# One pool of buffers, a more cautious planner, and another order of blocks in a two-layer encoder trunk

## The chip, the cores and the metric

The kernel runs on one core of a Trainium2 chip. Its work is issued to TensorE (PE: matmuls; PEld: their weight loads), VectorE (DVE), ScalarE (ACT) and SyncE (SP), which issues nearly all DMAs. GpSimd (POOL) does next to nothing. Each engine executes its instructions in the order in which they were written for it, and waits where an instruction's input or buffer isn't ready. The metric is device microseconds of one execution, as the median of several runs.

## The reference

`x` is (256, 2048) in float32, and there are two layers. Per layer (weights differ by layer):

```python
shift, scale, gate = split(c @ w_ada + b_ada, 3)          # c: (2048,), w_ada: (2048, 6144)
h = rms_norm(x, g_pre) * (1 + scale) + shift
u, g_pool, q, k, v, g_diff = split(h @ w_in)              # w_in: (2048, 6144), each part 1024 wide
pool_out = multiscale_pool(u, w_pool, pool_scale) * silu(g_pool)   # trailing means over 2, 4, 8, 16 tokens, 4 groups
q, k = rope(q), rope(k)
p = softmax(mask(q @ k.T / 8))                            # 8 heads, 2 maps each, chunks of 64 tokens
att = (p[0] - lam * p[1]) @ v
diff_out = rms_norm(att, subln_g) * (1 - lam_init) * silu(g_diff)
y = concat(pool_out, diff_out) @ w_out                    # w_out: (2048, 2048)
x = x + (1 + gate) * rms_norm(y, g_post)
```

All weights are float32 and are read once: about 50 MB of `w_ada`, 50 MB of `w_in` and 17 MB of `w_out` for each layer.

## The kernel before

**Products.** Each float32 operand is split into a high part (rounded to the matmul's format, `hi`) and a rest (`lo`), and a product is made of three matmuls, hi x hi, hi x lo and lo x hi. The unit of work is a piece of 256 rows of contraction by 512 columns of `w_in` or `w_out` (`Unit`, 512 KB): two 128-row halves, times two halves of the 256 tokens, times three matmuls, which is 12 matmuls of 128 x 512. For each unit SP loads `raw`, ACT casts `hi` (`cast`), and DVE subtracts to get `lo` (`rest`); tiles in the profile are `rawz`, `whiz`, `wloz`. The blocks of 512 columns of `w_in` are numbered 0 to 11: U 0 and 1, the pool's gate GP 2 and 3, Q 4 and 5, K 6 and 7, V 8 and 9, the attention's gate GD 10 and 11. GP blocks are computed turned (features on the partitions), in matmuls of 256 columns.

**The conditioning.** `w_ada` is no matmul: each half row tile of 128 x 1024 (`adaz`, 512 KB, 192 in all) is multiplied by the spread `c` and summed along the row by one DVE instruction (`ada`). When the sums of a column tile are there, `ab` makes A (the factor) and B (the summand) of `h` for it, and ACT writes the modulated `h` from the transposed, scaled `xn` (`make_h`; `half_h` for the first ones of a layer, by halves of the tokens). The contraction is in eight pairs of column tiles ("k pairs"), and `w_in` products can use a k pair only when its h is there.

**The plan.** `plan` lays out the units: a block is visited with as many k pairs as are then available, the partial sum is saved to SBUF and copied back into PSUM at the next visit (`prepare`: `accc<-zz` in the profile), and the blocks end in the order in which they complete, to which `ORDERS` gives their numbers. `w_out` goes through its four column blocks with one half of the contraction and then with the other (`HALVES`); contraction tiles 0 to 7 (k pairs 0 to 3) are the pool's outputs and 8 to 15 the attention's. `START` says how many k pairs of h a layer begins with, which also forces their `w_ada` tiles in ahead of it; `TURN` says how many first units are regrouped so that they are done for the first half of the tokens and then for the second.

**The order on the engines.** No loop runs on the chip: Python threads (`Task`) each write a part of the program, and `Flow` decides whose instruction comes next. It has a model of each engine's clock (`COST`: fixed, per element, for an accumulating output, until visible), of the DMA link (`MB_US`, `LANDING`, `FIRST`) and of TensorE's slow start (`COLD`). `next_of` takes, for an engine, the waiting instruction with the earliest due time among those that could start at once by the model:

```python
rows.append((t.due(), max(self.now[k], a.dep), us, t))
rows.sort(key=lambda r: r[:2])
```

Products are due at 1e9, after everything else; a transpose, a pool or an attention step is due some us ahead of the unit that needs it (`need`, `need_h`, `need_cat`). All instructions are recorded in helper line 126, so groups in the profile are told apart by tile names.

**Buffers.** There are 34 buffers of 128 x 1024 floats ("z") for `raw`, `hi`, `lo`, `w_ada` tiles, saved sums, h and cat; 12 of 128 x 512 ("t") for temporaries: xn and the unsplit h, the rotated q and k, the probabilities, their transposes, the pool's; and one of 128 x 2048 ("g") that holds `w_pool` and then the spread gate G. `Slots.take` waits in the plan until enough are free and takes the one that was last used longest ago. The instruction that first writes it then waits on the chip for the last user.

Of the kernel before, what the change touches and what calls it, by code (L numbers as in the profile page):

```python
# [130 lines left out]
class Flow:  # L131
# [6 lines left out]

    COST = {"vector": (0.07, 1.05e-3, 0.01, 0.13), "scalar": (0.085, 0.89e-3, 0.13, 0.15), "gpsimd": (0.25, 2.3e-3, 0.0, 0.15)}
    TABLES = ((AF.Exp, 1), (AF.Silu, 2), (AF.Sin, 3))  # L140
    TABLE_US = 1.29
    MB_US, LANDING, FIRST = 0.40, 1.6, 3.8
    COLD = (1.8, 4.0)
    NEAR = {"tensor": 0.0, "vector": 0.1, "scalar": 0.1, "gpsimd": 0.1, "sync": 0.0}

# [60 lines left out]
    def next_of(self, k, asks):  # L206

        rows = []
        for t in asks:
            a = t.ask  # L210
            if a.dep is None:
                a.dep = self.depends(a)
            us = a.us + self.TABLE_US * bool(a.table and a.table[0] != self.table)
            rows.append((t.due(), max(self.now[k], a.dep), us, t))
        rows.sort(key=lambda r: r[:2])
        t0 = min(r[1] for r in rows) + self.NEAR[k]
        for i, (due, at, us, t) in enumerate(rows):
# [135 lines left out]


class Kern:
    BIG, TMP, BANKS, ACCS = 34, 12, 4, 4

    def __init__(self, ctx, tc, a, out):
        f = self.f = self.nc = Flow(tc.nc)
        self.a, self.out = a, out  # L360
        pool = lambda name, **kw: ctx.enter_context(tc.tile_pool(name=name, bufs=1, **kw))
        self.cp, self.sp = pool("cp"), pool("sp")
        self.big = Slots(f, pool("zp"), "z", self.BIG, raw=3, hi=3, lo=3, ada=2)
        self.tmp = Slots(f, pool("tp"), "t", self.TMP)
        self.wide = Slots(f, pool("gp"), "g", 1)
        self.banks = Slots(f, pool("psp", space=PSUM), "b", self.BANKS)

# [18 lines left out]

    START = [1, 3]

    TURN = [3, 9]
    RATE = {(0, 2): 0.82, (1, 2): 0.85, (0, 0): 0.92, (0, 1): 0.9, (1, 0): 0.8, (1, 1): 0.35}  # L390
    ORDERS = [[6, 4, 7, 5, 2, 8, 9, 3, 10, 11, 0, 1]] * 2

    HALVES = ((4, 8), (0, 4))

# [136 lines left out]
    def begin(self):  # L531
# [11 lines left out]
        self.mod = [self.const([P, 2, 48], "mod") for l in range(DEPTH)]  # L543
        self.A = [self.const([P, KT], "A") for l in range(DEPTH)]
        self.B = [self.const([P, KT], "B") for l in range(DEPTH)]
        self.ones = self.const([1, P], "ones")
# [57 lines left out]
    def columns(self):  # L604

        v = self.nc.vector
        self.b1 = self.const([P, DEPTH, 32], "b1")
        v.tensor_scalar(self.b1, self.cols[:, :, 16:48], 1.0, None, op0=ALU.add)
        for l in range(DEPTH):
# [40 lines left out]
    def load_pool_weights(self, l):  # L650
        f, first = self.f, self.first_end[l]["w_in"]
        f.due(self.need(first, 30.0))
        f.wait(lambda: self.units[self.steps[self.at][0].visit.at].l == l and self.need(first)() < f.time + 60.0)
        wps = self.wide.take([P, 8, S], "Gw")
        for g in range(4):
            self.nc.sync.dma_start(wps[:, 2 * g : 2 * g + 2, :], self.a["w_pool"][l][:, 2 * g : 2 * g + 2, :])
        self.wps[l] = wps
# [124 lines left out]
    def ada(self):  # L782

        v = self.nc.vector
        for e in self.adas:
# [8 lines left out]
            self.big.give(w)  # L794
            if i and 16 <= nt < 32:
                self.ab(l, nt - 16)
                self.made[l] = nt - 15
            if i and nt == 47:
                self.f.spawn(lambda l=l: self.gate(l), self.need(self.first_end[l]["w_out"], 12.0))

    def ab(self, l, kt):
        v = self.nc.vector
        sl, m = slice(kt, kt + 1), self.mod[l]
        sc = slice(16 + kt, 17 + kt)
        v.scalar_tensor_tensor(self.A[l][:, sl], m[:, 0, sc], m[:, 1, sc], self.b1[:, l, sl], op0=ALU.add, op1=ALU.add)
        v.tensor_tensor(self.A[l][:, sl], self.A[l][:, sl], self.cols[:, l, 48 + kt : 49 + kt], op=ALU.mult)
        v.scalar_tensor_tensor(self.B[l][:, sl], m[:, 0, sl], m[:, 1, sl], self.cols[:, l, sl], op0=ALU.add, op1=ALU.add)

    def gate(self, l):
# [3 lines left out]
        nc.vector.tensor_tensor(col, self.mod[l][:, 0, 32:48], self.mod[l][:, 1, 32:48], op=ALU.add)  # L813
        nc.vector.tensor_tensor(col, col, self.b1[:, l, 16:32], op=ALU.add)
        nc.vector.tensor_tensor(col, col, self.cols[:, l, 64:80], op=ALU.mult)
# [36 lines left out]
    def modulated(self, out, l, kt, x):  # L852
        self.nc.scalar.activation(out, x, AF.Identity, bias=self.B[l][:, kt : kt + 1], scale=self.A[l][:, kt : kt + 1])

# [369 lines left out]
    def pool_group(self, l, g):  # L1224
# [18 lines left out]
        for dt in range(2):  # L1243
            for ct in range(2):
                nc.tensor.matmul(
                    m[:, dt * S : (dt + 1) * S], self.wps[l][:, 2 * g + ct, dt * P : (dt + 1) * P], pt[:, ct, :],
                    start=ct == 0, stop=ct == 1,
# [3 lines left out]
        if self.mixed[l] == 4:  # L1251
            self.wide.give(self.wps[l])
        for dt in range(2):
# [14 lines left out]
    def end_out(self, u, sts):  # L1268
# [7 lines left out]
        for st in sts:  # L1276
            if u.end:
                nc.scalar.activation(self.sqj, acc[st], AF.Square, accum_out=self.yss[l][:, st, nb : nb + 1])
                nc.vector.tensor_tensor(y[:, st, :], acc[st], self.G[l][:, nb * NB : (nb + 1) * NB], op=ALU.mult)
                self.gated[l][st] += 1  # L1280
# [6 lines left out]
        if self.gated[l] == [4, 4]:  # L1287
            self.wide.give(self.G[l])

# [69 lines left out]
```

## Time and profile before

| | |
|---|---|
| median of 3 runs | 872.72 us (870.72 to 877.0) |
| the profiled execution | 867.77 us, span 866.0 us |
| mean granted TensorE clock | 0.983 |
| HBM read | 242.17 MB, 282 GB/s over the span |
| first / last matmul of layer 0's w_in to w_out | about 19 to 436 us |
| the same of layer 1 | about 438 to 856 us |

The profile shows one execution. Busy time is the time that an engine spends in instructions; "idle before, releaser" says what ended the time in which it stood still. PE's "psb" are small matmuls and transposes into the four PSUM banks for things between products; "accc" and "accb" are the products' sums. In a row of the table of stages, instructions of each engine stand in brackets behind its busy time. The tail after 856 us is the last norm, the residual and the stores.

### The profile page before, as it was taken

What the parts mean: (1) busy time and instruction counts of PE and PEld (TensorE: products, weight loads), DVE (VectorE), ACT (ScalarE), POOL (GpSimd) and SP (SyncE); (2) the same over time, 40 slices, a digit from 0 to 9 for tenths busy, and PEclk for the clock granted to TensorE, in tenths of its full rate; (3) what the DMA queues carried; (4) which work ended last, traced back from release to release, by engine and by line L of the source; (5) the groups of instructions that cost most, each with busy time, mean ns of one, the idle gap of its engine ahead of it and who ended that gap; (6) DMA issues with size and microseconds to landing.
All of it is one profiled execution on the core that took longest, in us unless ns stands there. A gap on an engine that the chain in (4) does not pass through costs nothing. (4 is left out here: it accounts for less than half of the span.)

```text
span 866.0 us, 11893 instructions
## 1 busy us (share of the span) xinstructions
PE 810.9 (94%) x4058; PEld 669.4 (77%) x4058; DVE 714.7 (83%) x1314; ACT 529.9 (61%) x917; POOL 0.2 (0%) x4
## 2 busy tenths in 40 slices
PE   4899999989999999999979979999969999999995
PEld 1688878868778878888757868888857888888884
DVE  7999998788998999979998878788898867974524
ACT  5799986656566888535496444455455668844330
POOL 0000000000000000000000000000000000000000
PEclk9999999999999999999999989999979999999998
DMA  9999999998986993689867899999996565445502
GB/s 344 408 356 359 346 399 350 379 328 315 381 266 205 350 373 135 198 328 402 289 264 244 314 320 339 343 366 370 385 343 204 151 215 148 145 168 182 209 0 98
DMA packets 68671, 245.08 MB, mean 283 GB/s; under 512 B 7777, under 2 KB 8065, under 8 KB 68097
## 3 DMA queue, kind: packets, MB, share of 16 engines
q1 hardware_dynamic: 68322, 244.14, 78.5%
q8 instruction: 32, 0.52, 0.2%
q10 hardware_dynamic: 288, 0.17, 0.1%
q14 instruction: 29, 0.24, 0.1%
HBM read 242.17 MB, written 2.11 MB: 282 GB/s over the span
## 5 line engine op out<-in xcount | busy, mean ns | idle before, releaser
L126 PE MATMUL accc<-whiz,hz 128*128 128x512 f32 x1248 | 404.0, 399 | 8.4 <-ACT hz L126 6.3
L126 ACT CAST whiz<-rawz 128x1024 fp32r<-128x1024 f32 (+1 forms) x259 | 265.1, 1045 | 142.6 <-DVE wloz L126 52.5
L126 DVE TENSOR_TENSOR wloz<-rawz,whiz 128x1024 fp32r<-128x1024 f32 (+1 forms) x259 | 308.1, 1209 | 31.4 <-ACT whiz L126 22.2
L126 PEld LDWEIGHTS accc<-whiz,hz 128*128 128x128 f32 x1248 | 236.8, 191 | 61.7 <-ACT hz L126 7.9
L126 DVE SCALAR_TENSOR_TENSOR adaz<-adaz,cb 128x1024 f32<-128x1024 f32 x192 | 232.9, 1221 | 48.3 <-DMA adaz<-in_w_ada 45.7
L126 PE MATMUL accc<-wloz,hz 128*128 128x512 f32 x624 | 248.0, 398 | 0.0
L126 PE MATMUL accc<-whiz,catz 128*128 128x512 f32 x512 | 160.0, 391 | 1.5 <-ACT accc L126 1.5
L126 PEld LDWEIGHTS accc<-wloz,hz 128*128 128x128 f32 x624 | 119.3, 191 | 24.1 <-issue 0.8
L126 PEld LDWEIGHTS accc<-whiz,catz 128*128 128x128 f32 x512 | 96.1, 188 | 21.6 <-ACT accc L126 1.9
L126 PE MATMUL accc<-wloz,catz 128*128 128x512 f32 x256 | 99.9, 390 | 0.0
L126 PE MATMUL accc<-hz,whiz 128*128 128x256 f32 x512 | 75.8, 287 | 0.0
L126 ACT COPY accc<-zz 128x512 f32<-128x512 f32 x93 | 53.7, 603 | 27.9 <-DVE rtt L126 20.7
L126 PEld LDWEIGHTS accc<-hz,whiz 128*128 128x128 f32 x512 | 68.3, 193 | 2.0 <-issue 0.8
L126 ACT COPY zz<-accc 128x512 f32<-128x512 f32 x107 | 59.4, 593 | 14.4 <-PE accc L126 8.4
L126 PEld LDWEIGHTS accc<-wloz,catz 128*128 128x128 f32 x256 | 48.1, 188 | 9.9
L126 ACT ACTIVATE hz<-psb,B,A 128x256 fp32r<-128x256 f32 (+1 forms) x40 | 21.2, 530 | 38.2 <-DVE B L126 32.3
L126 PE MATMUL accc<-hz,wloz 128*128 128x256 f32 x256 | 42.0, 285 | 0.0
L126 PE MATMUL psb<-consts,xnt 128*128 128x128 f32 x64 | 13.8, 311 | 23.9 <-ACT xnt L126 19.6
L126 PEld LDWEIGHTS accc<-hz,wloz 128*128 128x128 f32 x256 | 35.5, 192 | 0.2
L126 ACT ACTIVATE pt<-psb,sm 128x128 f32<-128x128 f32 (+1 forms) x64 | 26.5, 421 | 12.1 <-DVE sm L126 8.1
L126 PEld LDWEIGHTS psb<-consts,xnt 128*128 128x128 f32 x64 | 7.9, 149 | 31.9 <-ACT xnt L126 26.0
L126 DVE TENSOR_TENSOR yz<-accc,Gwg 128x512 f32<-128x512 f32 x16 | 10.9, 688 | 23.7 <-ACT sqj L126 23.6
(112 smaller groups left out, 572.3 us busy)
## 6 DMA issues: line engine op xcount, KB each, us to landing
adaz<-in_w_ada SPq DMA_DIRECT2D x192, 512.0 KB, 6.9
rawz<-in_w_in SPq DMA_DIRECT2D x189, 512.0 KB, 5.9
rawz<-in_w_out SPq DMA_DIRECT2D x64, 512.0 KB, 5.0
x<-in_x SPq DMA_DIRECT2D x2, 1024.0 KB, 9.1
Gwg<-in_w_pool SPq DMA_DIRECT2D x8, 256.0 KB, 6.2
Gwg<-gate SPq DMA_DIRECT2D x2, 1024.0 KB, 4.6
out<-x SPq DMA_DIRECT2D x8, 256.0 KB, 2.8
rawz<-in_w_in SPq DMA_DIRECT2D x6, 256.0 KB, 8.7
```

Of the source, the lines that this page charges most:

```text
L126: return f(*args, **kw)
```

## The change

- *Model.* ACT and DVE get higher costs, a DMA a later landing and a lower rate, the link a slightly earlier first transfer.
- *Slack.* For TensorE, a step with a due time between 0 and 1e8 (all but products and a layer's first transposes) counts as startable only 1.5 us after the model's time for its input.
- *Due times.* Weight loads, casts, rests and the copies of partial sums are due 1.2 to 2 us earlier.
- *One pool.* 42 buffers of 128 x 1024 for all. Temporaries take halves of them (`Halves`). `w_pool` and G take two each in place of the one wide buffer; they come in two DMAs each, and G no longer waits for the pool groups.
- *Order.* The blocks end in the order GD 10, GP 2, GP 3, GD 11, K 6, Q 4, U 0, U 1, K 7, Q 5, V 8, V 9 (before: K 6, Q 4, K 7, Q 5, GP 2, V 8, V 9, GP 3, GD 10, GD 11, U 0, U 1). `w_out` begins with the pool's half of the contraction.
- *Second layer.* It begins with two k pairs in place of three, and six regrouped units in place of nine.
- *A and B.* They lie in one tile AB, and are made for two column tiles at once by three instructions (layer 0's first two column tiles one by one).

```diff
-    COST = {"vector": (0.07, 1.05e-3, 0.01, 0.13), "scalar": (0.085, 0.89e-3, 0.13, 0.15), "gpsimd": (0.25, 2.3e-3, 0.0, 0.15)}
+    COST = {"vector": (0.09, 1.08e-3, 0.02, 0.15), "scalar": (0.11, 0.92e-3, 0.13, 0.18), "gpsimd": (0.25, 2.3e-3, 0.0, 0.15)}
-    MB_US, LANDING, FIRST = 0.40, 1.6, 3.8
+    MB_US, LANDING, FIRST = 0.38, 2.4, 3.4
+    SLACK = 1.5
...
-            rows.append((t.due(), max(self.now[k], a.dep), us, t))
+            due = t.due()
+            slack = self.SLACK * (k == "tensor" and 0 < due < 1e8)
+            rows.append((due, max(self.now[k], a.dep + slack), us, t))
...
+class Halves:
+    def __init__(self, slots):
+        self.slots, self.flow, self.open, self.tiles = slots, slots.flow, [], {}
+
+    def take(self, shape, tag, dt=F32, n=None):
+        got = []
+        for _ in range(n or 1):
+            if not self.open:
+                x = self.slots.take([P, 2, 512], "half")
+                self.tiles[x.tensor.name] = x
+                self.open += [(x, 0), (x, 1)]
+            x, i = self.open.pop(min(range(len(self.open)), key=lambda j: self.rank(*self.open[j])))
+            v = x[:, i, 0 : math.prod(shape[1:])]
...
+    def rank(self, x, i):
+        return sum(y is x for y, _ in self.open), self.flow.latest(self.flow.used, self.flow.region(x[:, i]))
+
+    def give(self, *halves):
...
+            if other:
+                self.open.pop(other[0])
+                self.slots.give(x)
+            else:
+                self.open.append((x, i))
...
-    BIG, TMP, BANKS, ACCS = 34, 12, 4, 4
+    BIG, BANKS, ACCS = 42, 4, 4
...
-        self.tmp = Slots(f, pool("tp"), "t", self.TMP)
-        self.wide = Slots(f, pool("gp"), "g", 1)
+        self.tmp = Halves(self.big)
...
-    START = [1, 3]
-    TURN = [3, 9]
+    START = [1, 2]
+    TURN = [3, 6]
...
-    ORDERS = [[6, 4, 7, 5, 2, 8, 9, 3, 10, 11, 0, 1]] * 2
-    HALVES = ((4, 8), (0, 4))
+    ORDERS = [[10, 2, 3, 11, 6, 4, 0, 1, 7, 5, 8, 9]] * 2
+    HALVES = ((0, 4), (4, 8))
...
-        wps = self.wide.take([P, 8, S], "Gw")
-        for g in range(4):
-            self.nc.sync.dma_start(wps[:, 2 * g : 2 * g + 2, :], self.a["w_pool"][l][:, 2 * g : 2 * g + 2, :])
+        wps = self.big.take([P, 4, S], "wp", n=2)
+        for i, w in enumerate(wps):
+            self.nc.sync.dma_start(w, self.a["w_pool"][l][:, 4 * i : 4 * i + 4, :])
...
-            if i and 16 <= nt < 32:
-                self.ab(l, nt - 16)
-                self.made[l] = nt - 15
+            if i and 16 <= nt < 32 and (nt % 2 or not l and nt < 18):
+                kt = nt - 16
+                self.ab(l, kt if not l and kt < 2 else kt - 1, kt + 1)
+                self.made[l] = kt + 1
...
-    def ab(self, l, kt):
-        v = self.nc.vector
-        sl, m = slice(kt, kt + 1), self.mod[l]
-        sc = slice(16 + kt, 17 + kt)
-        v.scalar_tensor_tensor(self.A[l][:, sl], m[:, 0, sc], m[:, 1, sc], self.b1[:, l, sl], op0=ALU.add, op1=ALU.add)
-        v.tensor_tensor(self.A[l][:, sl], self.A[l][:, sl], self.cols[:, l, 48 + kt : 49 + kt], op=ALU.mult)
-        v.scalar_tensor_tensor(self.B[l][:, sl], m[:, 0, sl], m[:, 1, sl], self.cols[:, l, sl], op0=ALU.add, op1=ALU.add)
+    def ab(self, l, k0, k1):
+        v, ab = self.nc.vector, self.AB[l][:, :, k0:k1]
+        m, b = (x.rearrange(f"{p} (g k) -> {p} g k", k=KT) for x, p in ((self.mod[l], "p i"), (self.b1[:, l, :], "p")))
+        v.tensor_tensor(ab, m[:, 0, 0:2, k0:k1], m[:, 1, 0:2, k0:k1], op=ALU.add)
+        v.tensor_tensor(ab, ab, b[:, 0:2, k0:k1], op=ALU.add)
+        v.tensor_tensor(ab[:, 1], ab[:, 1], self.cols[:, l, 48 + k0 : 48 + k1], op=ALU.mult)
...
-        self.f.wait(lambda: self.mixed[l] == 4)
-        G = self.wide.take([P, D], "Gw")
-        nc.sync.dma_start(G, far.partition_broadcast(P))
+        G = self.big.take([P, 2, NB], "G", n=2)
+        for i, x in enumerate(G):
+            nc.sync.dma_start(x.rearrange("p b n -> p (b n)"), far[:, i * D // 2 : (i + 1) * D // 2].partition_broadcast(P))
...
-            self.f.due(self.need(u, 7.0))
+            self.f.due(self.need(u, 9.0))
...
-            self.f.due(-5.0 + 1.5 * ks.start if u.group == 1 else self.need(u, 1.5))
+            self.f.due(-5.0 + 1.5 * ks.start if u.group == 1 else self.need(u, 3.0))
...
-            self.f.due(-5.0 + 1.5 * ks.start if u.group == 1 else self.need(u, -0.2))
+            self.f.due(-5.0 + 1.5 * ks.start if u.group == 1 else self.need(u, 1.0))
...
-                self.f.due(self.need(u, 1.5 - st))
+                self.f.due(self.need(u, 3.5 - st))
```

More of the change, by code (lines that the diff above doesn't have):

```diff
@@ L352, in give @@
             self.count[kind] -= 1
+class Halves:
[10 more added lines that the diff above has]
+            v = x[:, i, 0 : math.prod(shape[1:])]
+            if dt != F32:
+                v = v.bitcast(dt)
+            names = "abcd"[: len(shape) - 1]
+            if len(names) > 1:
+                v = v.rearrange(f"p ({' '.join(names)}) -> p {' '.join(names)}", **dict(zip(names, shape[1:])))
+            got.append(v)
+        return got if n else got[0]
+    def rank(self, x, i):
+        return sum(y is x for y, _ in self.open), self.flow.latest(self.flow.used, self.flow.region(x[:, i]))
+    def give(self, *halves):
+        for v in halves:
+            name = v.tensor.name
+            i = int(self.flow.region(v)[3] >= 512)
+            x = self.tiles[name]
+            other = [j for j, (y, k) in enumerate(self.open) if y is x]
+            if other:
[3 more added lines that the diff above has]
+                self.open.append((x, i))
 class Kern:
-    BIG, TMP, BANKS, ACCS = 34, 12, 4, 4
+    BIG, BANKS, ACCS = 42, 4, 4
     def __init__(self, ctx, tc, a, out):
@@ L543, in begin @@
         self.mod = [self.const([P, 2, 48], "mod") for l in range(DEPTH)]
-        self.A = [self.const([P, KT], "A") for l in range(DEPTH)]
-        self.B = [self.const([P, KT], "B") for l in range(DEPTH)]
+        self.AB = [self.const([P, 2, KT], "AB") for l in range(DEPTH)]
         self.ones = self.const([1, P], "ones")
@@ L606, in columns @@
         v = self.nc.vector
-        self.b1 = self.const([P, DEPTH, 32], "b1")
-        v.tensor_scalar(self.b1, self.cols[:, :, 16:48], 1.0, None, op0=ALU.add)
+        self.b1 = self.const([P, DEPTH, 48], "b1")
+        v.tensor_copy(self.b1[:, :, 0:16], self.cols[:, :, 0:16])
+        v.tensor_scalar(self.b1[:, :, 16:48], self.cols[:, :, 16:48], 1.0, None, op0=ALU.add)
         for l in range(DEPTH):
@@ L813, in gate @@
         nc.vector.tensor_tensor(col, self.mod[l][:, 0, 32:48], self.mod[l][:, 1, 32:48], op=ALU.add)
-        nc.vector.tensor_tensor(col, col, self.b1[:, l, 16:32], op=ALU.add)
+        nc.vector.tensor_tensor(col, col, self.b1[:, l, 32:48], op=ALU.add)
         nc.vector.tensor_tensor(col, col, self.cols[:, l, 64:80], op=ALU.mult)
@@ L852, in modulated @@
     def modulated(self, out, l, kt, x):
-        self.nc.scalar.activation(out, x, AF.Identity, bias=self.B[l][:, kt : kt + 1], scale=self.A[l][:, kt : kt + 1])
+        self.nc.scalar.activation(out, x, AF.Identity, bias=self.AB[l][:, 0, kt : kt + 1], scale=self.AB[l][:, 1, kt : kt + 1])
     def make_h(self, l, kp):
@@ L1245, in pool_group @@
                 nc.tensor.matmul(
-                    m[:, dt * S : (dt + 1) * S], self.wps[l][:, 2 * g + ct, dt * P : (dt + 1) * P], pt[:, ct, :],
+                    m[:, dt * S : (dt + 1) * S], self.wps[l][half][:, 2 * gg + ct, dt * P : (dt + 1) * P], pt[:, ct, :],
                     start=ct == 0, stop=ct == 1,
@@ L1251, in pool_group @@
         if self.mixed[l] == 4:
-            self.wide.give(self.wps[l])
+            self.big.give(*self.wps[l])
         for dt in range(2):
@@ L1278, in end_out @@
                 nc.scalar.activation(self.sqj, acc[st], AF.Square, accum_out=self.yss[l][:, st, nb : nb + 1])
-                nc.vector.tensor_tensor(y[:, st, :], acc[st], self.G[l][:, nb * NB : (nb + 1) * NB], op=ALU.mult)
+                nc.vector.tensor_tensor(y[:, st, :], acc[st], self.G[l][nb // 2][:, nb % 2, :], op=ALU.mult)
                 self.gated[l][st] += 1
@@ L1287, in end_out @@
         if self.gated[l] == [4, 4]:
-            self.wide.give(self.G[l])
+            self.big.give(*self.G[l])
     def residual(self, l, st):
```

## The prediction

> **What bounds the kernel now.** I read the page's shares of busy time first, then a table of stages, then, stage by stage, the list of TensorE's own waits, and last the single stalls in order of time.
>
> ```profile
> span 866.0 us, 11893 instructions
> PE 810.9 (94%) x4058; PEld 669.4 (77%) x4058; DVE 714.7 (83%) x1314; ACT 529.9 (61%) x917; POOL 0.2 (0%) x4
> ```
> ```profile
> 32.00:118.00 86.00, 85.51 (x438) 72.65 (x437) 80.77 (x130) 78.06 (x129) 0.00 (x0) 1.00 0.97 367
> 118.00:218.00 100.00, 92.72 (x473) 78.09 (x472) 85.85 (x136) 67.20 (x102) 0.00 (x0) 0.98 0.96 349
> 218.00:334.00 116.00, 114.32 (x641) 93.36 (x640) 107.56 (x236) 83.26 (x182) 0.00 (x0) 1.00 0.87 314
> 334.00:430.00 96.00, 94.49 (x430) 78.05 (x430) 86.85 (x149) 48.13 (x66) 0.00 (x0) 1.00 0.72 263
> 430.00:458.00 28.00, 21.93 (x89) 16.22 (x88) 25.89 (x63) 24.35 (x57) 0.00 (x0) 0.94 0.64 244
> 458.00:560.00 102.00, 94.74 (x484) 80.56 (x483) 84.33 (x140) 51.59 (x75) 0.00 (x0) 0.97 0.91 321
> 560.00:628.00 68.00, 68.00 (x335) 57.75 (x335) 56.98 (x76) 34.29 (x44) 0.00 (x0) 1.00 1.01 374
> 628.00:650.00 22.00, 15.36 (x59) 12.04 (x58) 21.07 (x32) 11.25 (x13) 0.00 (x0) 0.77 0.94 343
> 764.00:856.30 92.30, 92.25 (x416) 76.59 (x414) 43.97 (x55) 33.84 (x48) 0.00 (x0) 1.00 0.41 137
> ```
>
> The columns of the table are the stretch and its length, then busy time and instructions of PE, PEld, DVE, ACT and POOL, the granted clock, the DMA share and GB/s. TensorE is busy in 94% of the span. Where nothing disturbs it (764 to 856) it is busy without a break and finishes 416 matmuls in 92.30 us, 0.222 us each. The products are the floor, and the change takes none of them away: only TensorE's idle time and its slow clock can be won. DVE is the next engine (80.77 of 86 us at 32 to 118, 21.07 of 22 us at 628 to 650), and the DMA rows are at 349 to 374 GB/s in three stages. Whatever takes out a stall has to be fed by these two.
>
> The waits of PE (total, times, longest) from 32 to 430 us, then in the turn between the layers (430 to 460), then from 460 on:
>
> ```profile
> PE psb L126 <- ACT xnt L126: 3.6, 4, 1.2
> PE psb L126 <- DVE xnt L126: 3.6, 1, 3.6
> PE accc L126 <- ACT accc L126: 1.5, 1, 1.5
> PE psb L126 <- DVE rtt L126: 0.9, 1, 0.9
> PE psb L126 <- DVE aTt L126: 0.7, 1, 0.7
> PE accc L126 <- DVE accc L126: 0.6, 1, 0.6
> ```
> ```profile
> PE psb L126 <- ACT xnt L126: 4.0, 2, 2.3
> PE accc L126 <- ACT hz L126: 1.0, 1, 1.0
> PE psb L126 <- ACT hft L126: 0.6, 1, 0.6
> ```
> ```profile
> PE psb L126 <- ACT xnt L126: 7.2, 2, 5.5
> PE psb L126 <- DVE rtt L126: 6.6, 2, 4.5
> ```
>
> So the body of the run (without start, turn and tail) has 10.9 + 13.8 = 24.7 us of idle TensorE in 13 stalls. 22.6 us of them are of one kind: "psb", a transpose that the plan put into TensorE's queue between products and whose input was not there yet, with products that could have run standing behind it. The other 2.1 us are products that wait for a partial sum copied back into PSUM.
>
> The two worst places, TensorE in order of time:
>
> ```profile
> 510.50 1.30 PE L126 MATMUL psb<-consts,xnt 128*128 128x128 f32 x4 [5.52 <-ACT xnt L126]
> 511.45 0.78 PE L126 MATMUL accc<-whiz,hz 128*128 128x512 f32 x1
> ...
> 514.16 1.72 PE L126 MATMUL accc<-hz,whiz 128*128 128x256 f32 x8
> ```
> ```profile
> 640.33 1.11 PE L126 MATMUL psb<-consts,rtt 128*128 128x128 f32 x4 [4.47 <-DVE rtt L126]
> 644.46 1.11 PE L126 MATMUL psb<-consts,rtt 128*128 128x128 f32 x4 [2.17 <-DVE rtt L126]
> ```
>
> After the stall of 5.52 us the six matmuls from the row at 511.45 up to the row at 514.16 (four rows left out) take 2.71 us, 0.45 each, twice the usual 0.222: the stall is paid a second time in clock. The granted clock bounds that from above: (1 - 0.98) x 100 + (1 - 0.97) x 102 + (1 - 0.77) x 22 = 2.0 + 3.1 + 5.1 = 10.2 us, which includes slow time that fell into the idle time itself. From below, six matmuls at 0.23 us too much behind each of the four stalls of over 2 us are 5.5 us. I take 6.
>
> Why the inputs are late, in the waits of the other engines:
>
> ```profile
> ACT whiz L126 <- DVE wloz L126: 52.5, 29, 3.9
> DVE adaz L126 <- DMA adaz<-in_w_ada: 45.7, 44, 3.2
> ACT hz L126 <- DVE B L126: 32.3, 13, 6.1
> ACT whiz L126 <- DVE adaz L126: 28.5, 20, 3.8
> ACT whiz L126 <- PE accc L126: 16.6, 14, 2.8
> ```
>
> DVE sits still for w_ada tiles that land later than planned (45.7 us), ACT sits still for the B that DVE then makes late (32.3 us), and the next xn is queued behind that on ACT. It is a chain of in-order queues that ends at TensorE. The three whiz rows are waits for a buffer or for its last reader.
>
> **The change part by part.**
>
> Slack. The planner now puts a step of TensorE between products only 1.5 us after it thinks the input is there. No instruction gets a new wait; products come first instead. A stall of up to 1.5 us goes: the four on ACT's xnt that make 3.6 together, and 0.9 and 0.7, 5.2 us. Of the five longer ones (3.6, 5.5, 7.2 - 5.5 = 1.7, 4.5, 6.6 - 4.5 = 2.1, in all 17.4) 1.5 each goes, 7.5 us, and 9.9 us are left. The cover is a product that is ready, and the row at 764 shows products running without help. Where h itself is missing there is no cover and the slack gives nothing.
>
> Costs, landing and due times. These change the order alone. Planned DVE and ACT times rise by about 5% (for 1,024 elements 1.145 to 1.196 and 0.996 to 1.052 us, by the formula), a DMA is expected 0.8 us later, casts, rests and sums are due 1.2 to 2 us earlier. At best the 9.9 us go too, at worst nothing, since real landings are late by up to 3.2 us. I take half, 5 us, as the 3.2 is more than twice the added 0.8. The sums that come back earlier take the 2.1 us of "accc" waits.
>
> Clock. Of the 6 us I take 3.5: two of the three longest stalls shrink by 1.5 us and more, one keeps most of its length. The Trainium skill's page "TensorE: Matmul & The Clock Gate", Part 1, says that the half clock comes after an idle window of about 3.4 us; by it the stalls of 3.6 and 4.5 us, cut by 1.5, would lose their slow time, and 4 of the 6 us would go instead of 3.5, 19.8 us in all instead of the 19.3 below. That agrees with the slow rows behind the 5.52 us stall.
>
> A and B by pairs. Rows by shape:
>
> ```profile
> L126 DVE SCALAR_TENSOR_TENSOR A<-mod,b 128x1 f32<-128x1 f32 x32 | 6.9, 217 | 0.5
> L126 DVE TENSOR_TENSOR A<-A,cols 128x1 f32<-128x1 f32 x32 | 5.0, 157 | 0.7
> L126 DVE SCALAR_TENSOR_TENSOR B<-mod,cols 128x1 f32<-128x1 f32 x32 | 6.8, 214 | 0.0
> L126 DVE TENSOR_TENSOR gcol<-mod 128x16 f32<-128x16 f32 x2 | 0.3, 170 | 0.0
> L126 DVE SCALAR_TENSOR_TENSOR adaz<-adaz,cb 128x1024 f32<-128x1024 f32 x192 | 232.9, 1221 | 48.3 <-DMA adaz<-in_w_ada 45.7 <-PE accc L126 1.1
> L126 ACT ACTIVATE hz<-psb,B,A 128x256 fp32r<-128x256 f32 x24 | 13.7, 570 | 33.6 <-DVE B L126 28.3 <-PE psb L126 5.3
> L126 ACT ACTIVATE xnt<-x,ry 128x256 f32<-128x256 f32 x31 | 14.6, 506 | 3.4 <-DVE ry L126 3.4
> ```
>
> 96 instructions of 18.7 us become 9 + 8 = 17 calls of 3 at about 0.17 us, 8.7 us: 10 us less of DVE, beside products, so nothing on the path. More follows from the order. An h pair is now begun when both its columns are there, not at the first, so ACT no longer sits in front of the second B (most of the 28.3 us), and what is queued behind, casts and the next xn, comes sooner; that is part of the 5 us above. In exchange two xn (1.0 us), the transposes and two writes of the first column (1.1 us) move behind the second column: h is 2 to 2.5 us later. The cover is the plan's own distance of three units from the last tile to the first use, 36 matmuls at 0.222 or 8 us. Nothing, then; 2 us for each pair that loses the cover.
>
> Gated blocks first.
>
> ```profile
> L126 ACT ACT_TABLE_LOAD x14 | 18.0, 1283 | 8.7 <-DVE sm L126 5.3 <-DMA cb<-in_c 2.8 <-PE accc L126 0.5
> ```
>
> The 14 table loads become perhaps 6 to 8, as all Silu comes ahead of Exp: some 8 to 10 us of ACT, hidden, because ACT has 83.26 of 116 us of work at 218 to 334. V ends last, so attention moves out of the end of w_in and under the first half of w_out, and the pool groups go the other way. At most two pairs of heads are open and both need V, so the last two pairs come wholly after the first V. DVE at 334 to 430 has 9 us free now. I reckon that the moved attention costs nothing there as long as w_ada tiles are done earlier, at 218 to 334, where the attention leaves room. The cover is thin: I add 4 us of new stalls (0 to 8; 8.2 us is what the rtt and aTt rows of this kind cost now).
>
> Start of the second layer with two k pairs, group of six. Six w_ada tiles fewer are forced in ahead of the turn (six times about 1.2 us of DVE, in a row where DVE has 25.89 of 28 us), but the products that cover the second half of the rows are 6 x 1.33 = 8 instead of 12 us (a step of six matmuls at 0.222 is 1.33). The turn loses 5.6 us in these rows; a gain of at most that, a loss of at most the 4 us of cover. I take nothing.
>
> One pool, G and w_pool in two tiles each. G no longer waits for the pool groups; it has the first half of w_out as cover, and a load that SP issues behind it comes one issue later, against a planned lead of nine instead of seven us. Nothing. Start and tail keep their order: nothing.
>
> Sum: 5.2 + 7.5 + 5 + 2.1 + 3.5 - 4 = 19.3 us off the profiled execution, which took 867.77 us (866.0 of span and 1.8 around it): 848.5. The median of the runs, 872.72, lies 4.95 above it. Forecast: **853 us**, with a range of its own of 845 to 862.
>
> **The rivals.**
>
> *The stalls only move.* The planner's mistakes come from landings, whose lateness (up to 3.2 us) is above both the 0.8 and the 1.5 us, and a new order brings new places. Then just the short stalls go, 5.2 + 2.1, less 4 of new ones: 872.7 - 3.3, about 869. For it: the longest stall is over three times the slack. Against: 9 of the 13 stalls are under 2 us.
>
> *The link holds layer 0.* From 32 to 218 us the kernel moves 86 us x 367 GB/s + 100 us x 349 GB/s, 66.5 MB. If the 349 GB/s of the second row were all there is, its stage could not shrink, and its idle time with its clock (100 - 92.72 = 7.3 and 2.0, about 9 us) stays: 862. At the 374 GB/s of the row at 560 it could shrink by 186 - 178 = 8 us, nearly all of it. The Trainium skill's page "DMA: Bandwidth & Descriptors", Specifications, gives a core about 358 GB/s of HBM, by which 66.5 MB take 186 us and nothing at all could be won here. The rows of 367 over 86 us and 374 over 68 us are above that figure, so the trace speaks against it as a ceiling.
>
> *Temporaries wait for buffers (slower).* xn, hf, the rotated heads and the probabilities now come from the 42 buffers that weights pass through, so their first write may wait for a product, a rest or a DMA that used the buffer last. The whiz rows show that price: 52.5 + 28.5 + 16.6 = 97.6 us over 259 casts, 0.38 us each. Some 60 temporaries a layer (18 to 20 for h, 16 rotated, 20 in attention, 4 in the pool groups and a few more) make 120 x 0.38 = 45 us. If two thirds reach TensorE, as xn does directly, the sum is 848.5 + 30 + 5, about 884. It decides from 19.3 / 120 = 0.16 us per temporary. Against it: the buffer that was idle longest is taken first, and eight more buffers are in the pool.
>
> **How the numbers follow.** Forecast 0.52, link 0.13, moved stalls 0.20, buffers 0.15. A measurement of this kernel tells about 1% from no change, so faster is below 864, slower above 881.4: forecast and link are faster (0.65), moved stalls the same (0.20), buffers slower (0.15). The range goes down to 838, where all 24.7 us, the 6 us of clock and 4 us of the turn are gone (872.7 - 34.7), and up to 877, above the moved stalls with their 8 us of new ones; the buffers stay out.
>
> **What would show it.** The waits of PE from 32 us on: psb rows for xnt and rtt of 3 us or less each if the slack works, and none over 3 us; granted clock of 0.98 and more in all stages of the body. DVE: 51 small AB instructions. ACT: fewer than 10 table loads. Slowed by buffers, xnt, rtt or pt rows would wait for PE accc or DVE wloz. The link rival would show as DVE adaz waits above 45.7 us at some 350 GB/s up to 218 us. A psb wait on aTt, or products that wait for wloz after the last V, would show the attention's move to be dearer than my 4 us; a turn with more than 10 us of idle TensorE would prove my nothing for the group of six wrong.

## The result and the profile after

The changed kernel takes **851.44 us** (median, 848.76 to 854.67) against 873.44 us before (median over the first three runs and a fourth beside it): a ratio of 0.9747, interval 0.9697 to 0.9798. It is faster, and 853 us were forecast. The profiled execution took 850.48 us, with a span of 848.7 us; the prediction's sum had come to 848.5 for this execution's time. The medians in this document leave out one execution, 889.62 us of the run u_link below, which fell in a slower state of the chip.

The page of the changed kernel, its span and its line of busy times:

```profile
span 848.7 us, 12034 instructions
PE 817.5 (96%) x4154; PEld 678.7 (80%) x4154; DVE 702.0 (83%) x1260; ACT 545.2 (64%) x945; POOL 0.2 (0%) x4
```

The stages of the changed kernel (columns as before; layer 0 now ends its `w_in` at 308 and its `w_out` at about 427 us, layer 1 its `w_in` at 735; the rows for 0 to 32, 218 to 308 and 735 us on are left out):

```profile
32.00:118.00 86.00, 85.83 (x421) 71.66 (x420) 79.08 (x121) 76.53 (x122) 0.00 (x0) 0.99 1.01 405
118.00:218.00 100.00, 100.00 (x495) 84.47 (x494) 93.23 (x137) 79.48 (x116) 0.00 (x0) 1.00 0.92 341
308.00:404.00 96.00, 95.44 (x496) 76.16 (x496) 84.98 (x203) 64.52 (x160) 0.00 (x0) 1.00 0.77 257
404.00:450.00 46.00, 42.68 (x221) 37.65 (x220) 29.70 (x74) 25.23 (x56) 0.00 (x0) 0.85 0.61 221
450.00:635.00 185.00, 185.00 (x919) 156.56 (x918) 152.24 (x216) 115.21 (x164) 0.00 (x0) 1.00 0.90 322
635.00:735.00 100.00, 97.19 (x560) 82.29 (x558) 89.68 (x145) 61.55 (x103) 0.00 (x0) 1.00 0.74 265
```

Waits of PE in the changed kernel, from 32 to 330 us, from 330 to 430 us (one wait, at the turn between the layers; from 430 to 460 us there is none), and from 460 to 850 us:

```profile
PE accc L126 <- ACT accc L126: 0.8, 2, 0.7
PE accc L126 <- DVE catz L126: 0.5, 1, 0.5
PE accc L126 <- DVE hz L126: 0.2, 1, 0.2
...
PE psb L126 <- ACT halfz L126: 3.2, 1, 3.2
...
PE psb L126 <- DVE halfz L126: 2.8, 2, 2.0
```

The body's idle TensorE fell from 24.7 to 1.5 + 2.8 = 4.3 us, the turn's from 5.6 to 3.2 (two rows of 0.3 and 0.2 us are not counted in the 5.6), and the granted clock is 0.99 to 1.00 in the stages of the body where it was 0.98, 0.97 and 0.77 in three. That alone would be some 26 us of the profiled execution (20.4 of idle time and about 6 of clock, the prediction's estimate). It got 17.3 us shorter. The rest was taken back by something that isn't a wait at all: TensorE was busy for 817.5 us where it had been for 810.9, and the page counts 4154 matmuls where there were 4058. By shape, before and then after:

```profile
L126 PE MATMUL accc<-hz,whiz 128*128 128x256 f32 x512 | 75.8, 287 | 0.0
L126 PE MATMUL accc<-hz,wloz 128*128 128x256 f32 x256 | 42.0, 285 | 0.0
```
```profile
L126 PE MATMUL accc<-hz,whiz 128*128 128x256 f32 x448 | 62.8, 283 | 0.0
L126 PE MATMUL accc<-hz,wloz 128*128 128x256 f32 x224 | 36.0, 283 | 0.0
L126 PE MATMUL accc<-hz,whiz 128*128 128x128 f32 x128 | 20.2, 309 | 0.1
L126 PE MATMUL accc<-hz,wloz 128*128 128x128 f32 x64 | 11.5, 310 | 0.0
```

96 products of 256 columns have become 192 of 128. The six regrouped units of layer 1 belong to the blocks that end second, third and fourth, which by the new order are GP 2, GP 3 and GD 11. GP is computed turned, and by halves of the tokens a turned matmul has 128 columns. In order of time, at the turn:

```profile
427.06 1.12 PE L126 MATMUL psb<-consts,halfz 128*128 128x128 f32 x4 [3.20 <-ACT halfz L126]
428.29 1.97 PE L126 MATMUL accc<-hz,whiz 128*128 128x128 f32 x8
...
437.74 1.05 PE L126 MATMUL accc<-hz,wloz 128*128 128x128 f32 x4
438.59 0.73 PE L126 MATMUL accb<-whiz,hz 128*128 128x512 f32 x1
...
441.01 1.00 PE L126 MATMUL accc<-hz,whiz 128*128 128x128 f32 x8
441.85 0.61 PE L126 MATMUL accc<-hz,wloz 128*128 128x128 f32 x4
442.29 1.06 PE L126 MATMUL accc<-hz,whiz 128*128 128x128 f32 x8
...
448.20 1.00 PE L126 MATMUL accc<-hz,whiz 128*128 128x128 f32 x8
```

Twelve short products take 442.29 - 441.01 = 1.28 us at full clock, 0.107 each, hardly less than one of 256 columns (0.120: twelve take 1.44 us in the run gp_none below, from 505.39 to 506.83 us). The first 48 take 438.59 - 428.29 = 10.3 us, 0.215 each, since they stand in the slow clock behind the stall of 3.20 us.

### The profile page after: what moved, and what is told of

The parts are those of the page before. It is cut to its first block, busy times and chain, and to the rows that moved or that the text cites. A ratio compares the mean times of both kernels' runs of the same rounds, so it can differ in the third digit from the quotient of the medians.

```text
span 848.7 us, 12034 instructions
## 1 busy us (share of the span) xinstructions
PE 817.5 (96%) x4154; PEld 678.7 (80%) x4154; DVE 702.0 (83%) x1260; ACT 545.2 (64%) x945; POOL 0.2 (0%) x4
## 4 chain that ended last, share of the span: by engine, by line
PE 59%; DVE 2%; DMA 1%; ACT 1%; issue 0%; DVEq 0%; ACTq 0%
PE accc L126 51%; PE psb L126 7%; DMA rawz<-in_w_in 1%; PE accb L126 1%; DVE halfz L126 0%; ACT whiz L126 0%; DVE adaz L126 0%; DVE wloz L126 0%; DVE x L126 0%; DVE yz L126 0%; ACT sqj L126 0%; ACT halfz L126 0%; DVE zz L126 0%; DVE ry L126 0%; DVE rh L126 0%
## 5 line engine op out<-in xcount | busy, mean ns | idle before, releaser
L126 DVE SCALAR_TENSOR_TENSOR adaz<-adaz,cb 128x1024 f32<-128x1024 f32 x192 | 231.6, 1221 | 23.6 <-DMA adaz<-in_w_ada 20.8
L126 PEld LDWEIGHTS accc<-wloz,hz 128*128 128x128 f32 x628 | 118.5, 189 | 24.7 <-DVE wloz L126 0.3
L126 ACT COPY zz<-accc 128x512 f32<-128x512 f32 x127 | 73.1, 587 | 34.9 <-PE accc L126 33.9
L126 PE MATMUL accc<-hz,whiz 128*128 128x256 f32 (+1 forms) x576 | 83.0, 289 | 0.1
L126 ACT COPY accc<-zz 128x512 f32<-128x512 f32 x107 | 63.3, 592 | 25.3 <-DVE halfz L126 20.9
L126 PEld LDWEIGHTS accc<-hz,whiz 128*128 128x128 f32 x576 | 77.3, 200 | 1.3 <-ACT hz L126 0.5
L126 PE MATMUL accc<-hz,wloz 128*128 128x256 f32 (+1 forms) x288 | 47.5, 289 | 0.0
L126 PE MATMUL psb<-consts,halfz 128*128 128x128 f32 x176 | 30.9, 281 | 10.8 <-ACT halfz L126 8.0
L126 DVE TENSOR_TENSOR yz<-accc,Gz 128x512 f32<-128x512 f32 x16 | 11.0, 690 | 34.5 <-ACT sqj L126 34.4
L126 ACT ACTIVATE sqj<-accc 128x512 bf16<-128x512 f32 x16 | 9.6, 597 | 46.1 <-PE accc L126 45.9
L126 PEld LDWEIGHTS psb<-consts,halfz 128*128 128x128 f32 x176 | 22.5, 143 | 20.0 <-ACT halfz L126 10.4
L126 ACT ACTIVATE halfz<-psb,sm 128x128 f32<-128x128 f32 x64 | 26.5, 421 | 11.6 <-DVE sm L126 8.0
```

What stands on the lines that cost most here:

```text
L126: return f(*args, **kw)
```

## The experiments

All times are medians; the ratio is to the kernel before, run on the same chip.

| run | edit, to the changed kernel unless said | us | ratio (95%) |
|---|---|---|---|
| u_slack | slack 0 | 855.94 | 0.9833 (0.9759 to 0.9907) |
| u_model | costs, link, due times old | 881.89 | 1.0146 (1.0063 to 1.0228) |
| u_cost | costs alone old | 853.25 | 0.9771 (0.9715 to 0.9826) |
| u_link | link alone old | 878.89 | 1.0070 (1.0046 to 1.0093) |
| u_land | landing alone old | 860.09 | 0.9837 (0.9779 to 0.9895) |
| u_due | due times alone old | 856.96 | 0.9819 (0.9781 to 0.9857) |
| b_link | *before*, with the new link alone | 848.10 | 0.9705 (0.9646 to 0.9765) |
| u_pool | 36 buffers and 12 half ones | 854.19 | 0.9754 (0.9686 to 0.9821) |
| u_order | blocks and halves old | 848.91 | 0.9756 (0.9697 to 0.9815) |
| gp_later | layer 1: GP third and fourth | 841.58 | 0.9657 (0.9594 to 0.9719) |
| gp_none | layer 1: GP first and fifth | 837.42 | 0.9591 (0.9565 to 0.9616) |
| u_start | three k pairs, nine units | 842.69 | 0.9629 (0.9572 to 0.9687) |

Each edit lets the planner write the whole program anew, so a part of any difference can be an accident of the new order. How large such an accident gets was not measured, as no edit without a meaning was run. A single difference of under 10 us from the changed kernel (u_slack, u_cost, u_land, u_due, u_pool) is therefore a weak sign; the large ones were found in more than one plan.

### Slack or model

```diff
-    SLACK = 1.5
+    SLACK = 0.0
```

> The changed kernel with the slack set back to 0, everything else as changed. Theory (the slack removes the psb stalls): some 8 to 13 us of psb waits of PE come back in the body, with 2 to 4 us of slow clock, about 861 us. Rival (the dearer costs, later landings and earlier due times do it, the slack only rides along): the body's waits stay under 8 us and the time within 851 to 855 us.

```diff
-    COST = {"vector": (0.09, 1.08e-3, 0.02, 0.15), "scalar": (0.11, 0.92e-3, 0.13, 0.18), ...}
-    MB_US, LANDING, FIRST = 0.38, 2.4, 3.4
+    COST = {"vector": (0.07, 1.05e-3, 0.01, 0.13), "scalar": (0.085, 0.89e-3, 0.13, 0.15), ...}
+    MB_US, LANDING, FIRST = 0.40, 1.6, 3.8
...
-            self.f.due(self.need(u, 9.0))
+            self.f.due(self.need(u, 7.0))
...
-            self.f.due(-5.0 + 1.5 * ks.start if u.group == 1 else self.need(u, 3.0))
+            self.f.due(-5.0 + 1.5 * ks.start if u.group == 1 else self.need(u, 1.5))
...
-            self.f.due(-5.0 + 1.5 * ks.start if u.group == 1 else self.need(u, 1.0))
+            self.f.due(-5.0 + 1.5 * ks.start if u.group == 1 else self.need(u, -0.2))
...
-                self.f.due(self.need(u, 3.5 - st))
+                self.f.due(self.need(u, 1.5 - st))
```

> The changed kernel with the old costs, link figures and due times; the slack stays. Theory: the 5 us that I gave the model come back plus part of the clock, about 858 us. Rival (the slack alone does it): 851 us within 3 us. Rival (the model does nearly all): 865 us or more.

Without the slack the time rose by 4.5 us, far less than the theory's 10 and just above the rival's range, and the intervals of the two kernels overlap. PE's psb waits from 32 us on are 3.4 + 0.5 + 3.5 + 2.1 = 9.5 us, against 6.0; in the body they rose by 3.2 us, not by 8 to 13. The profiled span is 7.8 us longer, and 5.4 of that isn't idle time: the same 4154 matmuls keep PE busy for 822.9 us instead of 817.5, as half clock at the turn lasted 27.3 us and not 13.6 (see the last section). Without the new model the time rose by 30.5 us, to 1.5% above the kernel before, slack, pool and order in place. The last rival is met: the model did nearly all. So it was taken apart.

### Which part of the model

```diff
-    COST = {"vector": (0.09, 1.08e-3, 0.02, 0.15), "scalar": (0.11, 0.92e-3, 0.13, 0.18), ...}
+    COST = {"vector": (0.07, 1.05e-3, 0.01, 0.13), "scalar": (0.085, 0.89e-3, 0.13, 0.15), ...}
```

> The changed kernel with the old costs of ACT and DVE alone. With costs, link and due times all old it took 882 us, 30 more than changed, so one of the three carries far more than I gave them together. Theory (landings are where the lateness begins: w_ada tiles land 6.8 us after their issue by the median, ACT and DVE instructions take what the old formula says): within 4 us of 851. Rival (a plan that is 5% too quick on ACT and DVE drifts until it is late by several us): 865 us or more.

```diff
-    MB_US, LANDING, FIRST = 0.38, 2.4, 3.4
+    MB_US, LANDING, FIRST = 0.40, 1.6, 3.8
```

> The changed kernel with the old link figures alone (0.40 MB per us, landing 1.6, first 3.8). Theory (landings): 865 us or more, DVE's adaz waits on DMA back to 40 us or more from 20.8, psb waits of PE for ACT back. Rival (costs or due times): within 4 us of 851.

```diff
-            self.f.due(self.need(u, 9.0))
+            self.f.due(self.need(u, 7.0))
...
-            self.f.due(-5.0 + 1.5 * ks.start if u.group == 1 else self.need(u, 3.0))
+            self.f.due(-5.0 + 1.5 * ks.start if u.group == 1 else self.need(u, 1.5))
...
-            self.f.due(-5.0 + 1.5 * ks.start if u.group == 1 else self.need(u, 1.0))
+            self.f.due(-5.0 + 1.5 * ks.start if u.group == 1 else self.need(u, -0.2))
...
-                self.f.due(self.need(u, 3.5 - st))
+                self.f.due(self.need(u, 1.5 - st))
```

> The changed kernel with the old due times of weight loads, casts, rests and sum copies alone. Theory (landings): within 4 us of 851, some accc waits of PE for the copied sums back. Rival (casts and loads that come 1.5 to 2 us too late are what held TensorE): 860 us or more, with waits for wloz or whiz in PE's list.

The three link figures alone cost 27.5 us (878.89 against 851.44); the costs 1.8, within the intervals; the due times 5.5, more than the theory's 4, at the edge of what these intervals tell. With the old link, the waits of the engines and of PE, and the clock:

```profile
DVE adaz L126 <- DMA adaz<-in_w_ada: 53.1, 46, 3.4
```
```profile
PE psb L126 <- ACT halfz L126: 15.3, 5, 4.8
PE accc L126 <- ACT hz L126: 5.3, 4, 4.4
PE psb L126 <- DVE gcol L126: 4.7, 1, 4.7
PE psb L126 <- DVE halfz L126: 4.6, 1, 4.6
PE accc L126 <- ACT accc L126: 4.5, 6, 2.2
```
```profile
core 0: 878.7 us, clock 0.973
```

and of the changed kernel:

```profile
DVE adaz L126 <- DMA adaz<-in_w_ada: 20.8, 24, 1.9
```
```profile
PE psb L126 <- ACT halfz L126: 8.0, 2, 4.8
PE accc L126 <- ACT hz L126: 5.4, 4, 3.3
PE psb L126 <- DVE halfz L126: 2.8, 2, 2.0
```

The link itself is no other: issue to landing of a w_ada tile has a median of 6.9 us with the old figures and 6.8 with the new. What differs is the place that the plan gives to the work behind it. The new figures are also not nearer to the chip in every part, only more cautious: from 32 to 118 us the link moved 405 GB/s in the changed kernel and 419 in u_link, above both planned rates (0.38 and 0.40 MB per us, which is 380 and 400 GB/s). The costs, on the other hand, did come nearer, against what the expectation of u_cost says: a cast of 128x1024 takes 1.053 us, 0.996 by the old formula and 1.052 by the new, and that changed next to nothing. PE's waits add up to some 38 us with the old link (rows under 3 us included) against 21, and (1 - 0.973) x 878.7 = 23.7 us of clock is lost against (1 - 0.987) x 848.7 = 11.0. The two differences are 17 and 13 us, and the profiled spans differ by 30.0 (878.7 and 848.7). PE's busy time says the same: the same 4154 matmuls take 830.7 us instead of 817.5, 13.2 more.

```diff
# the kernel before
-    MB_US, LANDING, FIRST = 0.40, 1.6, 3.8
+    MB_US, LANDING, FIRST = 0.38, 2.4, 3.4
```

> The kernel before with the new link figures alone (0.38, 2.4, 3.4); no slack, old costs, order, pool and due times. In the changed kernel the old link figures cost 28 us. Theory (what the planner believes of the link places TensorE's transposes, in any order of blocks and any pool): most of the change's gain is here too, 850 to 858 us, PE's psb waits of the body from 22.6 to under 10 us. Rival (the new figures pay only with the slack, the order and the shared pool around them): 866 us or more.

```diff
-    MB_US, LANDING, FIRST = 0.38, 2.4, 3.4
+    MB_US, LANDING, FIRST = 0.38, 1.6, 3.4
```

> The changed kernel with the old landing (1.6 in place of 2.4) alone; the rate stays 0.38 and the first transfer 3.4. Theory (the landing is the figure that matters, as the trace shows lateness at each tile): 870 us or more, as with all three old. Rival (the rate matters: 0.40 lets the planned link run ahead of the real one, tile by tile, and the lateness grows through a stage): within 5 us of 851.

Three numbers put into the kernel before take it to 848.1 us, as fast as the whole change as far as the intervals tell. DVE's waits for w_ada fall to 26.1 us, and PE's psb waits:

```profile
PE psb L126 <- ACT xnt L126: 17.6, 6, 6.5
PE psb L126 <- DVE zz L126: 1.7, 2, 1.3
PE psb L126 <- DVE rtt L126: 1.6, 2, 0.9
```

Of the first row 5.6 us are at the start and 6.5 at the turn, so the body holds 9.5 us in psb rows (with four rows of 0.4 us or less that aren't shown), where there were 22.6: theory met, with a time 2 us better than its range. The rival, that the figures pay only together with the rest, falls. The old landing alone cost 8.7 us, more than the rate rival allowed and less than the theory asked for; its interval and that of the changed kernel just overlap. The rate and the first transfer were not run apart, so how the other 19 us divide between them, or arise only with the landing, stays open.

The traces of all runs agree. PE's psb waits in the body come to 22.6, 19.2 and 17.4 us in the three kernels with the old link figures (before, u_model, u_link), though the last two have the slack; to 5.7 with the old landing alone; and to 9.5 or less in the ten with the new figures (b_link 9.5 and u_slack 6.0, which have no slack, 0.0 to 3.9 in the others). So the slack did little where the link figures were the old ones, and took a few us more where they were new.

### The shared pool

```diff
-    BIG, BANKS, ACCS = 42, 4, 4
+    BIG, BANKS, ACCS = 36, 4, 4
...
-        self.tmp = Halves(self.big)
+        self.tmp = Slots(f, pool("tp"), "t", 12)
```

> The changed kernel with 12 half buffers of their own for the temporaries again and 36 in the pool (the same memory; w_pool and G stay in the pool). Theory: sharing costs nothing and gains little, 851 us within 4 us. Rival (temporaries wait for buffers that weights used, the price that I put at 0.38 us each): 846 us or less without the sharing. Rival (the sharing lets loads run further ahead): 857 us or more, with more DVE waits for adaz from DMA.

854.19 against 851.44 us: no difference that these intervals tell. The rival that had carried my chance of a slower kernel falls, for taking the sharing away gained nothing. The third, a time of 857 us, isn't met either, though DVE's waits for w_ada did rise, from 20.8 to 34.8 us.

### The order, and the short products

```diff
-    ORDERS = [[10, 2, 3, 11, 6, 4, 0, 1, 7, 5, 8, 9]] * 2
-    HALVES = ((0, 4), (4, 8))
+    ORDERS = [[6, 4, 7, 5, 2, 8, 9, 3, 10, 11, 0, 1]] * 2
+    HALVES = ((4, 8), (0, 4))
```

> The changed kernel with the old order of blocks and the old halves of w_out. In the changed trace 192 matmuls of 128 x 128 stand at 428 to 460 us, since both GP blocks fall into the six regrouped units and are done by halves of the tokens; they cost about 10 us more than 96 of 256 columns. Theory: the order was worth nothing but this price, so the old one gives about 842 us, with no 128 x 128 product. Rival (gated blocks first is what keeps rope and attention from stalling TensorE): stalls on rtt and aTt of 8 us and more return, and the time is 850 us or more.

```diff
-    ORDERS = [[10, 2, 3, 11, 6, 4, 0, 1, 7, 5, 8, 9]] * 2
+    ORDERS = [[10, 2, 3, 11, 6, 4, 0, 1, 7, 5, 8, 9], [10, 11, 0, 2, 3, 6, 4, 1, 7, 5, 8, 9]]
```

> The changed kernel with another order in the second layer alone: GD 10, GD 11, U 0, GP 2, GP 3, K 6, Q 4, U 1, K 7, Q 5, V 8, V 9, so that no GP block is among the first three. Theory (the 128 x 128 products cost 10 us, as halves of a 256-wide matmul cost almost as much as the whole): no 128 x 128 product, TensorE's work 8 to 10 us less, about 842 us. Rival (the turn is bound by ACT and DVE work for h anyway, so the shorter products only turn into waits): idle time of TensorE at the turn rises by as much, 851 us within 3 us.

```diff
-    ORDERS = [[10, 2, 3, 11, 6, 4, 0, 1, 7, 5, 8, 9]] * 2
+    ORDERS = [[10, 2, 3, 11, 6, 4, 0, 1, 7, 5, 8, 9], [2, 10, 11, 6, 3, 4, 0, 1, 7, 5, 8, 9]]
```

> The changed kernel with the second layer's order GP 2, GD 10, GD 11, K 6, GP 3, Q 4, U 0, U 1, K 7, Q 5, V 8, V 9. The regrouped blocks of the second layer are the second to fourth that end, so with GP first and fifth neither is among them; in the run before this one GP 2 still was, which left 96 products of 128 x 128 and gave 841.6 us. Theory: none is left and another 5 us go, about 837 us. Rival (the first run's gain came from another arrangement of the turn, not from the short products): 841.6 us within 2 us.

Two, one and no GP block among the regrouped ones: 851.4, 841.6 and 837.4 us. (gp_later had been meant to leave none; the regrouped blocks are the second to fourth, not the first three, so one was left, and it makes the step between.) The time went down by 9.9 and by 4.2 us, 14.0 in all, with 192, 96 and none of the short products, and no wait took their place. TensorE was busy for 817.5, 809.9 and 805.8 us, that is 7.6 and 4.1 us less. The counts alone give 96 x 0.107 - 48 x 0.120 = 4.5 us for each step, and in the first one half clock at the turn also fell from 13.6 to 6.8 us, which is worth 3.4. Shapes and turn of gp_none:

```profile
L126 PE MATMUL accc<-hz,whiz 128*128 128x256 f32 x512 | 72.0, 283 | 0.0
L126 PE MATMUL accc<-hz,wloz 128*128 128x256 f32 x256 | 41.5, 284 | 0.0
```
```profile
426.79 1.12 PE L126 MATMUL psb<-consts,halfz 128*128 128x128 f32 x4 [3.12 <-ACT halfz L126]
428.03 0.80 PE L126 MATMUL accc<-whiz,hz 128*128 128x512 f32 x1
...
433.31 0.41 PE L126 MATMUL accb<-whiz,hz 128*128 128x512 f32 x1
433.56 0.39 PE L126 MATMUL accb<-wloz,hz 128*128 128x512 f32 x1
```

The turn of gp_none still has its stall of 3.12 us, but the clock is back at about 433 us, not at 441. **This kernel, 837.42 us, beats both**: 0.9591 of before, and 837.42 / 851.44 = 0.984 of the changed one.

The old order has no short products either, and took 848.91 us: it gains the 14 us and loses 11.5 elsewhere, among them PE waits for sums copied back (2.5 + 3.2 us in its list) and for cat (2.8). By this pair of kernels, gated blocks first, with the halves of `w_out` exchanged, was worth some 11 us, and the regrouping hid it. My theory that the order was worth only its price falls; the rival's time is missed by 1 us, and its stalls on the rotated q and k and on the transposed probabilities did not return.

### Start and turn

```diff
-    START = [1, 2]
-    TURN = [3, 6]
+    START = [1, 3]
+    TURN = [3, 9]
```

> The changed kernel with three k pairs at the start of the second layer and nine regrouped units again, the order as changed. The regrouped blocks are then the last three that end (Q 5, V 8, V 9), so no product of 128 x 128 is made, as in the kernel of 837.4 us, from which it differs by the start and turn. Theory (start and turn are worth nothing by themselves): 837 us within 3 us. Rival (six more w_ada tiles in front of the turn hold DVE up): 843 us or more, with PE waits at the turn and in w_out of layer 0. Rival (three k pairs save eight visits and cover the turn better): 833 us or less.

842.69 us, between theory and the first rival, and 5.3 above gp_none; its profiled execution took 839.64, that of gp_none 837.81. The two kernels also differ in the order of layer 1's blocks, which the expectation leaves out. Two k pairs are perhaps a little better than three; the runs don't settle it. u_start makes no short product either, and is 8.8 us faster than the changed kernel.

## Why the prediction was right

**Time and sign** were right, and the kind of loss too: psb stalls of TensorE and the slow clock behind them went from the body. That the time came within 2 us of the forecast is luck: the terms of the sum were sized wrongly, in both directions, and came out even.

- *Slack, 12.7 us of stalls.* Taking it out of the changed kernel cost 4.5 us. The step that failed is "A stall of up to 1.5 us goes", and 1.5 us of each longer one: with the slack but the old link figures 17.4 and 19.2 of the 22.6 us of psb waits were still there (u_link, u_model). It was the new link figures that took most of them, and few were left for the slack.
- *Costs, landing and due times, 5 us.* The term that was mis-sized most: 27.5 us by the link alone, 1.8 by the costs, 5.5 by the due times, 30.5 together. I had argued from the longest wait for a w_ada tile (3.2 us) that 0.8 us more of planned landing could not reach it. But it could: landing alone cost 8.7 us, all three figures 27.5. By which steps a landing planned less than 1 us earlier comes to cost that much was not traced.
- *Clock, 3.5 of 6 us.* In the profiled execution the body's clock is now 1.00 to within a hundredth, so nearly all of it went. But at the turn half clock now lasts 13.6 us, where it lasted 3.4.
- *accc waits, 2.1 us.* 1.5 us of such product waits are left, at other places, so next to nothing was won.
- *New stalls, -4 us.* Wrong in kind. The attention under `w_out` cost PE 0.5 us of waiting for cat, and DVE found room for it, with 84.98 of 96 us busy there. What came was TensorE's own work: it took 14 us, slow clock included, to the kernel without the short products. The step that failed is the first one: "the products are the floor, and the change takes none of them away". It did not ask whether the change adds any; the code had the answer, in the regrouped units and the turned GP blocks.
- *The turn, nothing.* Its idle time fell by 2.4 us, but the slow clock fell on short products. I had put the cover for the second half of the tokens at 8 us; with four turned units of six it is 448.20 - 428.29 = 20 us (48 short products at half clock, 48 more after 441 us, and 12 of 512 columns).
- *A and B.* 51 instructions of 157 to 164 ns, 8.1 us, where I had 8.7. ACT's waits for B are gone from the list's head; yet b_link, which keeps 34.3 us of them, is as fast, so there they had cover. The part was not run alone.
- *Table loads.* 6, as the low end of my 6 to 8.
- *Link rival.* Fell: 405 GB/s from 32 to 118 us. The Trainium skill's page "DMA: Bandwidth & Descriptors", Specifications, gives about 358 GB/s for a core; this row stands 13% above it, for 86 us.
- *Moved stalls* fell with 4.3 us of idle time in the body, *buffers* with u_pool. One of the signs was missed: a psb wait of 3.20 us at the turn, where none over 3 us was to be left.

## What to carry to other kernels

Where a program's order is written from a model, try the model's figures group by group and alone, those first for what starts each chain, here the loads: three numbers did as much as all the edits together. Here the more cautious figures for the link were worth far more than the more exact ones for ACT's casts. And when an order changes, count each engine's instructions by shape before and after, not its waits alone: work that grows shows in no list of waits.

## What was not expected of the hardware

The slow clock behind a stall of much the same length lasted very differently. Stretches of the changed kernel (stall of 3.20 us, then products of 128 columns) and of gp_none (3.12 us, then 512 columns):

```profile
428.00:441.00 13.00, 12.88 (x55) 12.25 (x55) 9.13 (x21) 8.14 (x20) 0.00 (x0) 0.51 0.68 278
```
```profile
427.00:434.00 7.00, 6.88 (x19) 5.10 (x19) 6.03 (x11) 6.56 (x19) 0.00 (x0) 0.55 1.02 418
```

It was half for 13.6 us around the first and for 6.8 around the second, though TensorE was busy without a break behind both stalls. The Trainium skill's page "TensorE: Matmul & The Clock Gate", Part 1, gives about 3.4 us of sustained work until the full clock; the second is near two such windows, the first is four. The other traces bear the difference out. In the eight kernels whose products behind the turn's stall are the short ones (the changed kernel, u_slack, u_model, u_cost, u_link, u_land, u_due, u_pool), half clock lasted 13.6 us four times, and 17.1, 17.1, 20.5 and 27.3 us. In the six where they have 512 columns (before, b_link, u_order, u_start, gp_later, gp_none) a stretch of it lasted 3.4 or 6.8 us. The length of the stall doesn't sort them: the longest single one was 2.2 to 5.7 us in the eight and 2.3 to 6.5 in the six, and all stretches are near multiples of 3.4 us. Once the clock is full, stretches made mostly of short products don't bring it down:

```profile
441.00:461.00 20.00, 20.00 (x164) 19.29 (x163) 12.74 (x20) 9.01 (x17) 0.00 (x0) 1.00 0.39 118
```

So in these traces a TensorE that is busy with short products keeps its full clock but is slow to get it back. That it is the shape that does it, and not something else in these plans, was not tried apart from this place.
